# A third score bank, a deeper ring of weight loads, and work issued in another order, in a hybrid attention block

## Chip, cores and metric

One core of one Trainium2 chip runs the whole kernel. The metric is device time in microseconds (us), the median over runs. TensorE is the matrix engine, VectorE, ScalarE and GpSimd (POOL in the profile) work on tiles, SyncE (SP) issues most transfers.

## What is computed

```python
# D_MODEL 1024, SEQ 1024 + 16 meta tokens = L 1040, 8 heads of 64, float32
h    = rmsnorm(concat(meta, x), norm_g)
proj = h @ w_in      # u_pool, z_pool (512 each), q, k, v, z_attn (512 each), f_logit (8), g_pool, g_attn (1024 each)
y_pool = causal_multiscale_pool(u_pool, pool_w, pool_scale) * silu(z_pool)   # windows 2, 4, 8, 16
log_f  = log_sigmoid(f_logit + b_forget)
# logit[t, s] = q_t.k_s / 8 + sum of log_f over s < j <= t, causal, softmax over s
y_attn = forgetting_attention(q, k, v, log_f) * silu(z_attn)
merged = sigmoid(g_pool) * (y_pool @ w_up_pool) + sigmoid(g_attn) * (y_attn @ w_up_attn)
out = rmsnorm(x + merged @ w_out, final_norm_g)          # meta positions dropped
```

## The kernel before

Every float32 product is made of three: operands are split into a high and a low part (`hh`/`hl` for the activations, `whi`/`wlo` or `gw` for weights), and high x high, high x low and low x high are added up in one PSUM bank. A weight is loaded into a raw tile by SyncE's queue, copied to its high part by ScalarE (L157, L973) and subtracted to its low part by GpSimd or VectorE (L159, L978, L975).

**Attention stage.** There are 16 units: 4 pairs of heads (p), 2 heads of a pair (e), 2 halves of the queries. A unit of the first half has 5 blocks of 128 keys, one of the second half 9. `Unit.qk(b)` makes a score block: two products into a bank `ps` (L691, L692), VectorE adds bias and mask where the causal edge cuts the block (L698), ScalarE adds the bias elsewhere (L700), and VectorE keeps a running maximum (L705). `maxes` turns the maximum round (L710 to L723). `Unit.soft(b)` subtracts it (L732), exponentiates (L733), splits the result into `ph` and `pl` (L736, L737) and, two blocks later, `av` multiplies with V (L753). The score blocks of unit i + 1 are merged with the softmax blocks of unit i, so a phase holds either 5 softmax and 9 score blocks or 9 and 5.

Between these steps TensorE is given projections from a list, the fill (class `Fill`, `F.pull(ns)`): must-do ones (q, k and v of the next pair, `f_q`, `f_k`, `f_v`, `v_blocks`, with a `gate` that names the first unit in which they may start, and `apart`, which lets one go only behind a free one) and free ones (`f_u`, `f_raw`, results to DRAM through `st`, L343 and L353). `merged` pulls, after every step, `PACE * dve - pe` ns of fill, where the steps' `dve` is the planner's cost formula. A fill product is 24 matmuls into one bank of the pool `pj` (L171; V's transposes, L301, take a bank too); it is emptied by ScalarE and VectorE (L258/L262 for q, L281/L285 for k, L290 for v, L310/L311 for V's blocks). TensorE's order is the order of the program; the other engines' queues are ordered by a scheduler ahead of time, and each engine works through its queue in order. PSUM has 8 banks: `pj` 3, `psT` 2, `psS` 2 (scores), `psO` 1.

While attention runs, SyncE and GpSimd also add weight blocks in DRAM (`SUMS`, `put`, `add`) for the next stage. Behind unit 13 the first weights of that stage are loaded (`g_raw0`, L590), behind unit 14 they are split (L830, L833).

**Seven-product stage.** z_attn, z_pool and 512 columns of g_attn are projected by a two-by-two block scheme that takes seven block products (n = 0 to 6) of sums of blocks in place of eight; each has six column tiles i of 128, so there are 42 products in the list `order` (L1016). In the loop over `order`, step x splits the weights of product x + 4 (`split_next`, `w_split`), issues product x + 2 (`g_prod`), runs `before`, empties product x - 1 (`evict`: copies L1021, additions L1027, GpSimd additions L137, silus L1024), and runs what the table `extra` lists for it: sums of the softmax denominators (`acc_sum`, L934, L935, loads L929), `sums_in`, `sums_out`, steps of the pooling sums (`pool_chain`, L905), loads of attention results (`attn_in`) and of their reciprocals (`rc_in`, L883), `attn_norm` (L886), `h_split`, `pool_split` (L919, L920). In this loop all engines keep the order of the program. A raw weight tile holds two products' columns (`pair_in`, L961); two are in flight, and the next is loaded when both halves of one are split. The last four products alternate with `pool_mm`, the pooling mixer's product, whose banks come from the pool `p8`. The up projections (L171 again) and the output product (L1317) follow.

Of the kernel before, what the change touches and what calls it, by code (L numbers as in the profile page):

```python
# [8 lines left out]
F32 = mybir.dt.float32  # L9
# [13 lines left out]
KB = 128  # L23
# [8 lines left out]
HALVES = ((0, 512), (512, 1024))  # L32
PJ, PT = 3, 2
PACE = 1.0
LATENCY = 1800.0
# [20 lines left out]
def tile_hybrid_block(ctx, tc, x, meta, norm_g, w_in, b_forget, pool_w, pool_scale,  # L56
# [109 lines left out]
    def g_mm3(ps, terms):  # L166
# [3 lines left out]
        for i, (a, b) in enumerate(seq):  # L170
            nc.tensor.matmul(ps, a, b, start=(i == 0), stop=(i == len(seq) - 1))  # L171
            yield mm_ns(n)

    def g_proj(w, t0, t1):
        wh, wl = w
        ps = pj.tile([128, 512], F32, name="pj")[:, :t1 - t0]
        yield from g_mm3(ps, [(wh[:, k, :], wl[:, k, :], hh[k][:, t0:t1], hl[k][:, t0:t1]) for k in range(KO)])
        return ps
# [117 lines left out]
    def v_blocks(p, *parts):  # L296
        pt = pj.tile([128, 4, 2, 64], F32, name="pj")
        n = 0
        for b0, b1 in parts:
            for b in range(b0, b1):  # L300
                nc.tensor.transpose(pt[:, n], VT[p][:, KS[b]:KS[b] + KB], ident)  # L301
                n += 1
                yield 109.0
        for e in range(2):
            n = 0
            for b0, b1 in parts:
                pv = pt[:, n:n + b1 - b0]
                n += b1 - b0
                vh = V[p, e][:, b0:b1, e, :]
                nc.scalar.activation(vh, pv[:, :, e, :], AF.Copy)  # L310
                nc.vector.tensor_tensor(V[p, e][:, b0:b1, 1 - e, :], pv[:, :, e, :], r32(vh), op=ALU.subtract)  # L311
# [156 lines left out]
    for n, (kind, t0, t1) in enumerate(todo):  # L468
# [187 lines left out]
    class Unit:  # L656
# [9 lines left out]
        def a_steps(self):  # L666
            for b in range(self.nb):
                w = 512 - self.c0[b]
                yield w, 1.05 * w + 165 + 300 * (b * KB + KB > self.t0), 2 * mm_ns(w), (lambda b=b: self.qk(b))

        def c_steps(self):
            for b in range(self.nb):
                w = 512 - self.c0[b]
                yield w, 2.6 * w + 376, 2 * mm_ns(w), (lambda b=b: self.soft(b))

        def qk(self, b):
            p, e, q0, t0, kb, c0 = self.p, self.e, self.q0, self.t0, self.kb[b], self.c0[b]
# [12 lines left out]
            k0 = KS[b]  # L690
            nc.tensor.matmul(ps[:kb, c0:], ka[:, k0:k0 + kb], qa[:, q0 + c0:q0 + 512], start=True, stop=False)  # L691
            nc.tensor.matmul(ps[:kb, c0:], ka[:, k0:k0 + kb], ql[:, q0 + c0:q0 + 512], start=False, stop=True)  # L692
            nb_ = negc[:kb, b, h:h + 1]
            f0 = max(d1, c0)
            if d1 > c0:
                j = t0 + c0 - b * KB
                mk = tail if own_keys else mask[:, j:j + d1 - c0]
                nc.vector.scalar_tensor_tensor(s[:kb, c0:d1], ps[:kb, c0:d1], nb_, mk, op0=ALU.add, op1=ALU.add)  # L698
            if f0 < 512:
                nc.scalar.activation(s[:kb, f0:], ps[:kb, f0:], AF.Identity, bias=nb_)  # L700
# [107 lines left out]
    for i, u in enumerate(units):  # L808
# [40 lines left out]
    def bank():  # L849
        cnt[0] += 1  # L850
        return (pj if cnt[0] % 2 else p8).tile([128, 512], F32, name="pj")

    cnt = [0]
# [104 lines left out]

    def pair_in(n, q):
        raw_w[n, q] = wp.tile([128, 4, 256], F32, name="graw", tag="raw")  # L960
        nc.sync.dma_start(raw_w[n, q], rows_of(gsrc(n, q)))  # L961

# [35 lines left out]

    ga_ = [pool.tile([128, 512], F32, name=n) for pool, n in ((pj, "pj"), (pj, "pj"), (pj, "pj"), (psT, "pt"))]
    gb_ = [pool.tile([128, 512], F32, name=n) for pool, n in ((p8, "pj"), (p8, "pj"), (p8, "pj"), (psT, "pt"))]  # L1000
# [27 lines left out]

    later = []

# [10 lines left out]
    def evict(e):  # L1041
        n, i = e
        ps = onto[e]
        if i < 4:
# [53 lines left out]
    pair_in(*pairs.pop(0))  # L1098
    h_in(2)
# [6 lines left out]
    def split_next(e):  # L1106
        w_split(e)
        q = e[0], "aabbgg"[e[1]]
        halves[q] = halves.get(q, 0) + 1
        if halves[q] == 2 and pairs:  # L1110
            pair_in(*pairs.pop(0))

# [7 lines left out]
    def pad_hq():  # L1120
        hq.tile([128, SEQ], F32, name="wpad", tag="w")
        hq.tile([128, SEQ], F32, name="pad", bufs=1)

    def steps_of(g):
        return lambda: next(g, None)
# [6 lines left out]
    extra = {  # L1132
        (0, 0): [lambda: acc_sum(0), lambda: u_in(1)],
        (0, 1): [lambda: acc_sum(1), lambda: h_in(3)],
        (0, 2): [lambda: acc_sum(2), lambda: u_in(0)],
        (0, 3): [lambda: acc_sum(3)],
        (0, 5): [lambda: acc_sum(4)],
        (1, 1): [lambda: acc_sum(5), lambda: attn_in(0)],
        (1, 4): [lambda: acc_sum(6), lambda: attn_in(1)],
        (1, 5): [lambda: acc_sum(7), sums_in],  # L1140
        (2, 0): [lambda: h_split(3), lambda: h_in(5), lambda: attn_in(2)],
        (2, 1): [steps_of(c2_), lambda: attn_in(3)],
        (2, 2): [steps_of(c2_), sums_out],
        (2, 3): [steps_of(c2_)],
        (2, 4): [steps_of(c2_)],
        (2, 5): [steps_of(c1_), lambda: rc_in(0), lambda: rc_in(1)],
        (3, 0): [steps_of(c1_)],
        (3, 1): [lambda: h_split(4), lambda: h_in(6)],
        (3, 2): [steps_of(c1_), steps_of(c0_)],
        (3, 3): [steps_of(c0_), lambda: pool_split(3)],  # L1150
        (3, 4): [lambda: attn_norm(0)],
        (3, 5): [lambda: pool_split(2)],
        (4, 1): [lambda: h_split(5)],
        (4, 3): [lambda: pool_split(1)],
        (4, 4): [lambda: rc_in(2)],
        (5, 3): [lambda: h_split(6), lambda: attn_norm(1), lambda: rc_in(3)],
        (5, 2): [lambda: attn_norm(2)],
        (5, 1): [lambda: attn_norm(3), lambda: silu(za[0][:, T0_], za[0][:, T0_])],
        (5, 0): [lambda: pool_split(0), lambda: silu(za[1][:, T0_], za[1][:, T0_])],
        (5, 4): [lambda: silu(za[2][:, T0_], za[2][:, T0_]), lambda: silu(za[3][:, T0_], za[3][:, T0_])],  # L1160
    }
# [3 lines left out]
    for x, e in enumerate(order[:38]):  # L1165
# [7 lines left out]
        for f in before.get(e, ()):  # L1173
            f()
        if x:
            evict(order[x - 1])
# [39 lines left out]

    ws, rows_ = {}, {}
    ws[0, 0] = up_weights(0, 0)
    for n, i in enumerate((3, 2, 1, 0)):
# [88 lines left out]
    bk = [pool.tile([128, 512], F32, name=n) for pool, n in  # L1308
          ((pj, "pj"), (pj, "pj"), (pj, "pj"), (psT, "pt"), (p8, "pj"), (p8, "pj"), (p8, "pj"), (psT, "pt"))]
    ba, bb_ = bk[:4], bk[4:]  # L1310
# [126 lines left out]
```

## Time and profile before

| | us |
|---|---|
| median of 3 runs | 755.03 (754.86 to 755.35) |
| the profiled execution | 757.81 |
| its span, first to last instruction | 756.1 |
| TensorE busy | 720.1 |
| VectorE, ScalarE, GpSimd busy | 522.1, 425.5, 328.5 |
| attention stage, first to last score product | 82.9 to 414.3 |
| seven-product stage, first to last product | 446.3 to 585.6 |
| output product | 672.7 to 749.1 |

The first part of the profile's page gives the busy time of each engine; the list of waits names, for an engine's idle time, the instruction that ended it. A line of a timeline has start, length, engine, line, operation, output<-inputs and count, and in brackets the idle time ahead of it and what ended that. PE is TensorE, DVE VectorE, ACT ScalarE, SPq SyncE's queue.

### The profile page before, as it was taken

The page shows a single profiled execution, that of the slowest core. Times are in us where ns is not written, and L with a number is a line of the kernel's source. Part 1 is how long each engine was busy: PE and PEld are TensorE (multiplying, and loading weights), DVE is VectorE, ACT ScalarE, POOL GpSimd, SP SyncE. Part 2 cuts the span into 40 slices and gives each one's busy share as a digit, 9 for nine tenths or more (in the row PEclk, how much of TensorE's full clock was granted, in tenths as well). Part 3 has the DMA queues.
Part 4 walks back from the last instruction along what each step waited for, and adds up shares of the span by engine and source line. Part 5 has one row for each costly group of instructions (what it writes and reads, how often), then busy time and mean ns, then how long its engine had stood idle before and what let it go on. Part 6 is the DMA issues. An engine that isn't in the chain of part 4 may idle for free. (4 is left out here: it accounts for less than half of the span.)

```text
span 756.1 us, 10866 instructions
## 1 busy us (share of the span) xinstructions
PE 720.1 (95%) x3613; PEld 613.7 (81%) x3613; DVE 522.1 (69%) x917; ACT 425.5 (56%) x944; POOL 328.5 (43%) x417
## 2 busy tenths in 40 slices
PE   9999999999999999899996999999859999999996
PEld 6997989998979879797885888877737888888885
DVE  5643667786886868877773967767466744787775
ACT  7653576676866768676664634335343623526355
POOL 5422238485474845475464743335516001005243
PEclk9999999999999999999998999999988999999999
DMA  9211226958959597767787869685333656672006
GB/s 305 50 29 29 56 77 211 276 177 206 312 133 290 141 256 196 182 168 206 173 223 206 203 216 340 214 263 172 98 98 125 237 190 229 216 278 91 0 1 222
DMA packets 97226, 134.08 MB, mean 177 GB/s; under 512 B 11569, under 2 KB 62769, under 8 KB 94914
## 3 DMA queue, kind: packets, MB, share of 16 engines
q1 hardware_dynamic: 93360, 112.42, 46.6%
q0 software_dynamic: 2512, 18.35, 12.9%
q10 hardware_dynamic: 1298, 2.63, 0.9%
q8 instruction: 28, 0.46, 0.2%
q14 instruction: 28, 0.23, 0.1%
HBM read 103.29 MB, written 62.59 MB: 219 GB/s over the span
## 5 line engine op out<-in xcount | busy, mean ns | idle before, releaser
L171 PE MATMUL pj<-hh,whi 128*128 128x512 f32 (+3 forms) x576 | 130.1, 353 | 0.2 <-DVE V L311 0.2
L171 PE MATMUL pj<-hh,wlo 128*128 128x512 f32 (+3 forms) x576 | 129.6, 348 | 0.1
L171 PE MATMUL pj<-hl,whi 128*128 128x512 f32 (+3 forms) x576 | 128.6, 346 | 0.0
L171 PEld LDWEIGHTS pj<-hh,whi 128*128 128x128 f32 x576 | 98.3, 192 | 10.8 <-PE pj L301 0.4
L171 PEld LDWEIGHTS pj<-hh,wlo 128*128 128x128 f32 x576 | 96.3, 189 | 9.3 <-POOL wlo L435 0.3
L159 POOL TENSOR_TENSOR wlo<-raw,whi 128x256 fp32r<-128x256 f32 x100 | 75.5, 794 | 64.9 <-ACT whi L157 25.4
L171 PEld LDWEIGHTS pj<-hl,whi 128*128 128x128 f32 x576 | 96.0, 188 | 8.8
L737 DVE TENSOR_TENSOR pl<-S,ph 128x512 fp32r<-128x512 f32 (+4 forms) x112 | 87.0, 792 | 11.2 <-ACT ph L736 10.5
L745 POOL TENSOR_TENSOR acc<-acc,S 128x272 f32<-128x272 f32 (+4 forms) x80 | 77.5, 969 | 15.9 <-ACT S L733 11.1
L978 POOL TENSOR_TENSOR gw<-graw,gw 128x256 fp32r<-128x256 f32 x52 | 46.1, 910 | 70.9 <-ACT gw L973 56.9
L1016 PE MATMUL pj<-gh,gw 128*128 128x512 f32 x276 | 66.8, 397 | 5.0 <-ACT gw L973 2.4
L705 DVE TENSOR_TENSOR pt<-pt,S 128x400 f32<-128x400 f32 (+2 forms) x96 | 46.8, 487 | 33.8 <-ACT S L700 31.3
L700 ACT ACTIVATE S<-ps,negc 128x400 f32<-128x400 f32 (+2 forms) x96 | 48.7, 515 | 33.2 <-DVE S L698 31.5
L1016 PEld LDWEIGHTS pj<-gh,gw 128*128 128x128 f32 x276 | 51.5, 188 | 19.0 <-ACT gw L973 3.7
L736 ACT ACTIVATE ph<-S 128x512 fp32r<-128x512 f32 (+4 forms) x112 | 52.4, 480 | 8.8 <-PE po L753 7.7
L733 ACT ACTIVATE S<-S 128x512 f32<-128x512 f32 (+4 forms) x112 | 50.1, 478 | 10.6 <-DVE S L732 10.5
L691 PE MATMUL ps<-qa,ka 128*128 128x512 f32 (+4 forms) x112 | 37.9, 338 | 14.3 <-ACT S L700 14.1
L732 DVE TENSOR_TENSOR S<-S,pt 128x512 f32<-128x512 f32 (+4 forms) x112 | 50.5, 498 | 0.6
L973 ACT ACTIVATE gw<-graw 128x512 fp32r<-128x512 f32 x38 | 23.3, 624 | 39.7 <-DMA graw<-gs 19.0
L1211 DVE TENSOR_TENSOR rl<-pj,rl 128x512 f32<-128x512 f32 x32 | 21.9, 689 | 26.7 <-PE pj L171 26.0
L691 PEld LDWEIGHTS ps<-qa,ka 128*128 128x128 f32 x112 | 21.4, 191 | 21.2 <-ACT S L700 18.9
L692 PE MATMUL ps<-ql,ka 128*128 128x512 f32 (+4 forms) x112 | 38.1, 340 | 0.0
(239 smaller groups left out, 1396.0 us busy)
## 6 DMA issues: line engine op xcount, KB each, us to landing
raw<-in_w_in_dram SPq DMA_DIRECT2D x27, 512.0 KB, 4.5
gs<-gs POOLq DMA_DIRECT2D x4, 1536.0 KB, 11.4
graw<-gs SPq DMA_DIRECT2D x12, 512.0 KB, 4.0
gs<-in_w_in_dram SPq DMA_DIRECT2D x5, 1024.0 KB, 9.9
td<-in_w_out_dram SPq DMA_DIRECT2D x5, 1024.0 KB, 12.9
graw<-in_w_in_dram SPq DMA_DIRECT2D x9, 512.0 KB, 6.3
xt<-in_x_dram SPq DMA_DIRECT2D x8, 512.0 KB, 7.2
accd<-acc SPq DMA_DIRECT2D x16, 256.0 KB, 3.4
```

What stands on the lines that cost most here:

```text
L159: ins = nc.gpsimd.tensor_tensor(lo[:, k:k + 2], raw[:, k:k + 2], r32(hi[:, k:k + 2]), op=ALU.subtract)
L171: nc.tensor.matmul(ps, a, b, start=(i == 0), stop=(i == len(seq) - 1))
L691: nc.tensor.matmul(ps[:kb, c0:], ka[:, k0:k0 + kb], qa[:, q0 + c0:q0 + 512], start=True, stop=False)
L700: nc.scalar.activation(s[:kb, f0:], ps[:kb, f0:], AF.Identity, bias=nb_)
L705: nc.vector.tensor_tensor(m[:kb, c0:], m[:kb, c0:], s[:kb, c0:], op=ALU.max)
L732: nc.vector.tensor_tensor(s[:kb, c0:], s[:kb, c0:], self.pm[:kb, c0:], op=ALU.subtract)
L733: exps.append(nc.scalar.activation(s[:kb, c0:], s[:kb, c0:], AF.Exp))
L736: nc.scalar.activation(ph[:kb, c0:], s[:kb, c0:], AF.Copy)
L737: dves.append(nc.vector.tensor_tensor(pl[:kb, c0:], s[:kb, c0:], r32(ph[:kb, c0:]), op=ALU.subtract))
L745: accs.append(nc.gpsimd.tensor_tensor(acc[:kb, c0:], acc[:kb, c0:], s[:kb, c0:], op=ALU.add))
L978: nc.gpsimd.tensor_tensor(op[:, 1, k:k + 2], raw[:, k:k + 2], r32(op[:, 0, k:k + 2]), op=ALU.subtract)
L1016: nc.tensor.matmul(ps, stat(n, i, p, k), op_h[n][q][k // 2][:, k % 2], start=fresh and m == 0, stop=m == 11, skip_group_check=True)
```

## The change

Banks: `pj` has 2 banks, a new pool `pk` has 1. Every third score block takes `pk`, two of three `psS`. Before the attention stage the fill takes `pk` at every third product; in it (`spare[0] = False`), the fill has the 2 banks of `pj`. The pools of the later stages take `pk` where they took the third bank of `pj`.

Attention: ScalarE's part of a score block is issued ahead of VectorE's masked part. `PACE` and the planner's formulas have other constants. `f_k` is `apart`. `g_raw0` is loaded behind unit 12.

Seven-product stage: weight loads are issued whenever a raw tile is free (`pairs_in`); from step (2, 0) on there are two more raw tiles, in the space of the `hq` pool. The silus of `zp` are issued some steps later (`defer`; `run_due(x)` stands in step x between `before` and `evict`). The denominators' sums, the steps of the pooling sums, `attn_in`, `rc_in`, `attn_norm` and the silus of `za` stand at other steps.

```diff
-PJ, PT = 3, 2
-PACE = 1.0
+PJ, PT = 2, 2
+PACE = 1.05
...
+    pk = ctx.enter_context(tc.tile_pool(name="pk", bufs=1, space=PS))
...
+    turn, spare = [0], [True]
+    def third(pool, name):
+        turn[0] += 1
+        if turn[0] % 3 == 0:
+            return pk.tile([128, 512], F32, name="pj")
+        return pool.tile([128, 512], F32, name=name)
+    def fill_bank():
+        return third(pj, "pj") if spare[0] else pj.tile([128, 512], F32, name="pj")
...
+    spare[0] = False
...
-                yield w, 1.05 * w + 165 + 300 * (b * KB + KB > self.t0), 2 * mm_ns(w), (lambda b=b: self.qk(b))
+                yield w, 0.8 * w + 110 + 250 * (b * KB + KB > self.t0), 2 * mm_ns(w), (lambda b=b: self.qk(b))
...
-                yield w, 2.6 * w + 376, 2 * mm_ns(w), (lambda b=b: self.soft(b))
+                yield w, 2.8 * w + 390, 2 * mm_ns(w), (lambda b=b: self.soft(b))
...
-            ps = psS.tile([128, 512], F32, name="ps")
+            ps = third(psS, "ps")
...
+            if f0 < 512:
+                nc.scalar.activation(s[:kb, f0:], ps[:kb, f0:], AF.Identity, bias=nb_)
             if d1 > c0:
                 ...
                 nc.vector.scalar_tensor_tensor(s[:kb, c0:d1], ps[:kb, c0:d1], nb_, mk, op0=ALU.add, op1=ALU.add)
-            if f0 < 512:
-                nc.scalar.activation(s[:kb, f0:], ps[:kb, f0:], AF.Identity, bias=nb_)
...
-            F.add(f"k{p}", f_k(p))
+            F.add(f"k{p}", f_k(p), apart=True)
...
-        if i == 13:
+        if i == 12:
             g_raw0 = [...]
...
-    def pair_in(n, q):
-        raw_w[n, q] = wp.tile([128, 4, 256], F32, name="graw", tag="raw")
-        nc.sync.dma_start(raw_w[n, q], rows_of(gsrc(n, q)))
+    room, homes = ["raw", "raw"], {}
+    def pairs_in():
+        while pairs and room:
+            e = pairs.pop(0)
+            homes[e] = tag = room.pop(0)
+            raw_w[e] = (wp if tag == "raw" else hq).tile([128, 4, 256], F32, name="graw", tag=tag)
+            nc.sync.dma_start(raw_w[e], rows_of(gsrc(*e)))
...
+    def defer(k, f):
+        due.append((clock[0] + k, f))
+    def run_due(x):
+        clock[0] = x
+        for d in [d for d in due if d[0] <= x]:
+            due.remove(d)
+            d[1]()
...
-                silu(zp[i][:, T0_], zp[i][:, T0_], -1.0)
+                defer(3, lambda: silu(zp[i][:, T0_], zp[i][:, T0_], -1.0))
...
-                silu(zp[i][:, T1_], zp[i][:, T1_], -1.0)
+                defer(1, lambda: silu(zp[i][:, T1_], zp[i][:, T1_], -1.0))
...
-        if halves[q] == 2 and pairs:
-            pair_in(*pairs.pop(0))
+        if halves[q] == 2:
+            room.append(homes[q])
+            pairs_in()
...
+    def more_room():
+        room.extend(("w", "w"))
+        pairs_in()
```

The table `extra`, step by step (c2, c1, c0 are steps of the pooling sums, one each):

| what | before | after |
|---|---|---|
| acc_sum 0 to 4 | (0,0) (0,1) (0,2) (0,3) (0,5) | (0,1) (0,2) (0,3) (0,4) (0,5) |
| acc_sum 5, 6, 7 | (1,1) (1,4) (1,5) | (1,4) (1,5) (2,0) |
| sums_in, sums_out | (1,5), (2,2) | (2,0), (2,4) |
| more_room | none | (2,0) |
| c2 | (2,1) (2,2) (2,3) (2,4) | (0,0) (0,1) (2,1) (2,2) |
| c1 | (2,5) (3,0) (3,2) | (2,2) (2,3) (2,4) |
| c0 | (3,2) (3,3) | (3,0) (3,2) |
| attn_in 0 to 3 | (1,1) (1,4) (2,0) (2,1) | (1,1) (1,5) (2,1) (2,4) |
| rc_in 2, 3 | (4,4) (5,3) | (4,2) (4,4) |
| attn_norm 1 | (5,3) | (4,0) |
| silu of za 0, 1, 2, 3 | (5,1) (5,0) (5,4) (5,4) | (5,0) (5,4) (5,4) (6,4) |

More of the change, by code (lines that the diff above doesn't have):

```diff
@@ L296, in v_blocks @@
     def v_blocks(p, *parts):
-        pt = pj.tile([128, 4, 2, 64], F32, name="pj")
+        pt = fill_bank().rearrange("p (n e d) -> p n e d", e=2, d=64)
         n = 0
@@ L850, in bank @@
         cnt[0] += 1
-        return (pj if cnt[0] % 2 else p8).tile([128, 512], F32, name="pj")
+        return ((pj, p8, pj, p8, pk, p8)[cnt[0] % 6]).tile([128, 512], F32, name="pj")
     cnt = [0]
@@ L997, in stat @@
         return op_w[n, i][:, p, k]
-    ga_ = [pool.tile([128, 512], F32, name=n) for pool, n in ((pj, "pj"), (pj, "pj"), (pj, "pj"), (psT, "pt"))]
+    ga_ = [pool.tile([128, 512], F32, name=n) for pool, n in ((pj, "pj"), (pj, "pj"), (pk, "pj"), (psT, "pt"))]
     gb_ = [pool.tile([128, 512], F32, name=n) for pool, n in ((p8, "pj"), (p8, "pj"), (p8, "pj"), (psT, "pt"))]
@@ L1027, in plus_ @@
         return nc.vector.tensor_tensor(dst, ps, dst if a is None else a, op=ALU.add)
-    later = []
+    later, due, clock = [], [], [0]
+    def defer(k, f):
[5 more added lines that the diff above has]
+            d[1]()
     def g_store(j, half, src):
@@ L1142, in tile_hybrid_block @@
[L1142 to L1147, printed above, removed]
+        (0, 0): [steps_of(c2_), lambda: u_in(1)],
+        (0, 1): [steps_of(c2_), lambda: acc_sum(0), lambda: h_in(3)],
+        (0, 2): [lambda: acc_sum(1), lambda: u_in(0)],
+        (0, 3): [lambda: acc_sum(2)],
+        (0, 4): [lambda: acc_sum(3)],
@@ new lines, in tile_hybrid_block @@
+        (0, 5): [lambda: acc_sum(4)],
+        (1, 1): [lambda: attn_in(0)],
+        (1, 4): [lambda: acc_sum(5)],
+        (1, 5): [lambda: acc_sum(6), lambda: attn_in(1)],
+        (2, 0): [more_room, lambda: acc_sum(7), lambda: h_split(3), lambda: h_in(5), sums_in],
+        (2, 1): [steps_of(c2_), lambda: attn_in(2)],
+        (2, 2): [steps_of(c2_), steps_of(c1_)],
+        (2, 3): [steps_of(c1_)],
+        (2, 4): [steps_of(c1_), sums_out, lambda: attn_in(3)],
+        (2, 5): [lambda: rc_in(0), lambda: rc_in(1)],
@@ L1156, in tile_hybrid_block @@
-        (5, 3): [lambda: h_split(6), lambda: attn_norm(1), lambda: rc_in(3)],
+        (4, 4): [lambda: rc_in(3)],
+        (5, 3): [lambda: h_split(6)],
         (5, 2): [lambda: attn_norm(2)],
-        (5, 1): [lambda: attn_norm(3), lambda: silu(za[0][:, T0_], za[0][:, T0_])],
-        (5, 0): [lambda: pool_split(0), lambda: silu(za[1][:, T0_], za[1][:, T0_])],
-        (5, 4): [lambda: silu(za[2][:, T0_], za[2][:, T0_]), lambda: silu(za[3][:, T0_], za[3][:, T0_])],
+        (5, 1): [lambda: attn_norm(3)],
```

28 lines of the change are left out of this document (13 added, 15 removed).

## The prediction

> **What bounds the kernel now.** I read the page first, then the list of who waited for whom on TensorE, then a table of windows round each long wait, then the timelines of the five engines there. The page says that TensorE is the bound.
>
> ```profile
> span 756.1 us, 10866 instructions
> ...
> PE 720.1 (95%) x3613; PEld 613.7 (81%) x3613; DVE 522.1 (69%) x917; ACT 425.5 (56%) x944; POOL 328.5 (43%) x417
> ```
>
> No edit takes a matmul away, so only TensorE's idle time and its slow time can be won: 36 us idle, some of it before the first and behind the last matmul. The waits of TensorE, in total us, times and longest, show where it lies.
>
> ```profile
> PE ps L691 <- ACT S L700: 14.1, 9, 6.5
> PE pj L171 <- DVE gx L1027: 7.2, 1, 7.2
> PE pj L1016 <- ACT gw L973: 2.4, 2, 1.5
> PE pj L1016 <- DVE gx L1027: 1.5, 1, 1.5
> ...
> PE pj L1016 <- DVE zp L1027: 1.2, 1, 1.2
> ...
> PE pj L171 <- DVE V L311: 0.2, 1, 0.2
> ```
>
> Three places: score products (L691) that wait for ScalarE to empty a score bank, 14.1 us; the seven-product stage (L1016), 5.1 us; and one wait of 7.2 us at its end, before the pooling product (L171, pool_mm). Each large wait is followed by a stretch at half clock (the column after POOL's is the granted clock).
>
> ```profile
> 227.80:231.00 3.20, 3.18 (x9) 2.80 (x10) 2.10 (x3) 2.82 (x5) 1.86 (x4) 0.50 1.08 214
> 404.40:408.50 4.10, 4.10 (x10) 3.23 (x11) 2.08 (x3) 3.17 (x5) 4.10 (x7) 0.50 0.24 74
> 566.30:572.30 6.00, 5.98 (x14) 4.65 (x15) 1.72 (x3) 0.63 (x1) 5.57 (x8) 0.50 0.27 87
> ```
>
> Work done at 0.50 loses half of its stretch: 1.6, 2.0 and 3.0 us. So waits and clock together hold 33.2 us: 14.1 + 3.6 in attention, 12.3 + 3.0 in and just behind the product stage, 0.2 in the fill.
>
> **The change, part by part.**
>
> *First weights of the product stage loaded after unit 12, not 13.* The longest score wait is not about score banks:
>
> ```profile
> 392.70 0.40 SPq L590 DMA_DIRECT2D graw<-in_w_in_dram  x1
> ...
> 402.71 1.06 ACT L830 ACTIVATE gw<-graw 128x1024 fp32r<-128x1024 f32 x1 [5.76 <-DMA graw<-in_w_in_dram]
> 404.40 0.79 PE L691 MATMUL ps<-qa,ka 128*128 128x512 f32 x1 [6.55 <-ACT S L700]
> ```
>
> ScalarE's queue holds the copy L830 ahead of score evictions; it stands 5.76 us for a load issued 10 us before, and TensorE then stands 6.55 us. One unit earlier is some 20 us (next fence: 20.4 and 22.2 us for two units), twice the load's 10 us. The two loads pass unit 13's stores on SyncE's queue, 0.40 us of issue each, with nothing urgent behind them. The tiles they take belonged to pair 2, which is over. Gain 6.55 + 2.0 = 8.6 us.
>
> *Third score bank.* psS keeps two banks and every third tile goes to the new pk. Of the 14.1 us, 7.6 us in eight waits remain as true bank waits; the largest of them lie in the phases that run a short unit's softmax (5 blocks) beside a long unit's scores (9).
>
> ```profile
> 225.06 0.67 ACT L700 ACTIVATE S<-ps,negc 128x512 f32<-128x512 f32 x1
> 227.09 0.67 ACT L700 ACTIVATE S<-ps,negc 128x512 f32<-128x512 f32 x1
> 225.78 0.50 PE L691 MATMUL ps<-qa,ka 128*128 128x512 f32 x1 [1.32 <-ACT S L700]
> 227.82 0.79 PE L691 MATMUL ps<-qa,ka 128*128 128x512 f32 x1 [1.06 <-ACT S L700]
> ...
> 218.05:238.46 20.41, 18.03 (x83) 15.47 (x83) 13.27 (x29) 12.76 (x32) 11.01 (x15) 0.92 0.98 260
> 238.46:260.61 22.15, 22.15 (x122) 19.56 (x121) 18.24 (x36) 16.06 (x43) 14.79 (x15) 1.00 0.60 153
> ```
>
> Score 3 starts as eviction 1 ends (225.73), score 4 as eviction 2 ends (227.76). With three banks score 3 goes at once (225.78 - 1.32 = 224.46), and score 4, due about 0.7 us behind it (three products; eight take 1.98 us in the row at 353.17 below), is held by eviction 1 until 225.73: near 0.6 us instead of 2.4 here, 0.4 more if the shorter fill between scores is counted. Scaled to 7.6 us I leave 2.2. Gain 5.4 us and the 1.6 us of clock that came with 2.4 us of waits: 7.0 us, between 0 (ScalarE stays late at every block) and 9.2.
>
> The Trainium skill (TensorE: Matmul & The Clock Gate, HAM oscillation — how this bites in real kernels) says that the clock falls when TensorE idles longer than about 3.4 us. The first clock row disagrees: waits of 1.32 and 1.06 us were enough. By the page that 1.6 us would not hang on these waits, the gain would be 5.4 us and the time 734.5; I follow the row.
>
> *ScalarE ahead of the mask.* Both engines read the same bank.
>
> ```profile
> L700 ACT ACTIVATE S<-ps,negc 128x400 f32<-128x400 f32 (+2 forms) x96 | 48.7, 515 | 33.2 <-DVE S L698 31.5
> ```
>
> ScalarE now waits 31.5 us for VectorE's mask. Afterwards the mask waits for ScalarE, but the maximum follows it on VectorE with no further change of engine. The bank comes free after the same two operations, so I book 0 directly; the cover is VectorE's idle time (13.27 of 20.41 us busy, 18.24 of 22.15). If that is gone, the mask's wait moves into VectorE's queue and delays `pl` and the AV products.
>
> *Fill keeps two banks instead of three.* This is the price. A fill product may now start only when the last but one is emptied. Pairs of rows of the timeline: a product's first matmuls, and the last step of the eviction that would hold them.
>
> ```profile
> 77.55 0.60 ACT L258 ACTIVATE qa<-pj 64x512 fp32r<-64x512 f32 x1 [0.76 <-DVE ql L262]
> 77.95 1.37 PE L171 MATMUL pj<-hh,whi 128*128 128x384 f32 x7
> ...
> 160.26 0.50 PE L171 MATMUL pj<-hh,whi 128*128 128x272 f32 x2
> 161.54 0.48 ACT L290 ACTIVATE vt<-pj 128x384 f32<-128x384 f32 x1
> ...
> 210.59 0.85 PE L171 MATMUL pj<-hh,whi 128*128 128x512 f32 x3
> 212.34 0.56 DVE L285 TENSOR_TENSOR ka<-pj,ka 64x384 fp32r<-64x384 f32 x1
> ...
> 241.91 1.26 PE L171 MATMUL pj<-hh,whi 128*128 128x272 f32 x8
> 241.97 0.49 ACT L290 ACTIVATE vt<-pj 128x384 f32<-128x384 f32 x1
> ...
> 353.17 1.98 PE L171 MATMUL pj<-hh,whi 128*128 128x512 f32 x8
> 353.48 0.58 ACT L343 ACTIVATE st<-pj 128x512 f32<-128x512 f32 x1
> ```
>
> Overlaps: 0.20, 1.76, 2.31, 0.55, 0.89 us. The first and last pair are the first and last of 16 such in the attention stage; they add to 16.5 us, nearly all behind K's third piece and round V's short transposes. That is the upper end. The lower end takes the least lag seen (241.91: 0.55) at the three V's and nothing else: 2.5 us with the shorter overlaps behind them. Fewer banks cannot gain. `apart` on K puts a free product between Q and K and removes two (3.1 us), leaving 13.4. The rest comes in clusters, where a first wait lets ScalarE catch up before the second, and ScalarE loses its mask waits: I take 7 us, a bit over half.
>
> *Pace.* Per head the plan's sums go from 3736 + 6547 (scores) and 5374 + 12203 (softmax) to 3019 + 5201 and 5999 + 13658 ns: 27,860 against 27,877. The fill lasts as long; 0.7 us of it per unit moves from short-softmax to long-softmax phases. Cost 0, covered by VectorE's idle time above.
>
> *Product stage.* In its third column of products one weight load was late and nothing recovered.
>
> ```profile
> 488.89 1.93 SPq L944 DMA_DIRECT2D fin<-sums  x4
> ...
> 492.71 0.43 SPq L961 DMA_DIRECT2D graw<-gs  x1
> 500.67 0.63 ACT L973 ACTIVATE gw<-graw 128x512 fp32r<-128x512 f32 x1 [11.43 <-DMA graw<-gs]
> ...
> 551.82 0.63 ACT L1024 ACTIVATE zp<-zp 128x512 f32<-128x512 f32 x1 [6.02 <-DVE zp L1027]
> 557.16 1.49 DVE L886 TENSOR_TENSOR y<-y,rc 128x1024 f32<-128x1024 f32 x1 [2.86 <-DMA rc<-recs]
> 566.32 0.79 PE L171 MATMUL pj<-plh,pwh 128*128 128x512 f32 x1 [7.21 <-DVE gx L1027]
> ...
>   POOL zp L137: 12.1, 4
>   DVE zp L1027: 11.5, 4
> ```
>
> The load at 492.71 stood behind the softmax sums on SyncE and behind a two-buffer ring; ScalarE idled 11.43 us for it. From (2,0) on, two more raw tiles let loads run four products further ahead; what waits behind sums_in then is not needed for 10 us or more. The silus held ScalarE 12.1 + 11.5 us (last two rows, ScalarE's idle time before L1024), with the next weight splits queued behind them; issued three products (zp's first half) or one (second half) later, they find their sums ready. rc_in(2) and rc_in(3) move two products ahead and attn_norm(1), which frees the tile that rc_in(3) takes, six; so the 2.86 us for rc go. One silu of za moves from (5,1) to (5,0), one to (6,4): the same 0.6 us each, later in ScalarE's queue. The sums go one to two products later and the pool chains earlier on VectorE, with no instruction added; POOL's queue keeps its order. The chain that kept VectorE from emptying gx's bank, and pool_mm from starting, is made of these waits. Of 12.3 + 3.0 us I leave 1.8: VectorE gets the last sums, h_split(3) and both pool chains within five products. Gain 13.5 us, between 5.1 (the waits named L1016 alone) and 15.3. The other banks (ga_, bk, bank) keep their number.
>
> **Sum.** The profiled execution took 757.81 us (span 756.1 and 1.7 round it): 757.8 - 8.6 - 7.0 + 7.0 - 13.5 = 735.7. The median of the three runs, 755.03, stands 2.8 us lower; so 732.9.
>
> **The rivals.**
>
> *Bank cycling in the fill.* The 16.5 us are paid in full and two clusters trip the clock as at 227.8 (1.6 us each): 732.9 + 9.5 + 3.2 = 745.6. For it: the evictions' order is fixed in advance; only 0.2 us of fill wait appeared with three banks. Against: `apart` and ScalarE's freed 31.5 us. The Trainium skill, same page (A second HAM failure mode: psum-queue depth-cycling), tells of a kernel whose short idles at each bank change kept tripping the clock; the first clock row agrees that short waits can.
>
> *The product stage keeps its wait.* VectorE falls behind at (2,0) to (2,4), the bank for (3,2) is late again (1.5) and half of 7.2 + 3.0 stays: 6.6 instead of 1.8, 737.7.
>
> *The swap only turns the wait round.* VectorE, standing for ScalarE, delays evictions as much as the bank saves: 9.2 instead of 2.2 remain, 739.9. The Trainium skill (PSUM — Partial Sum Buffer, PSUM bank collisions raise a hardware error) has two engines on one bank kept apart in time whichever comes first; the 31.5 us row agrees.
>
> *All of it works.* Fill 2.5, nothing left in scores or products: 732.9 - 4.5 - 2.2 - 1.8 = 724.4.
>
> *Slower.* The fill's bank waits must exceed 29 us, the 29.1 of gains; with every overlap doubled because ScalarE's new order puts evictions last, 33 us: 758.9. Nothing but the fixed order speaks for it.
>
> **How the numbers follow.** Forecast 0.45 (728 to 738), bank cycling 0.20, product stage 0.13, swap 0.08, all of it 0.11, slower 0.03. 722 to 748 reaches over all but the last and the tails. A measurement of this kernel tells 0.2% (1.5 us) from no change; nothing but a mix of all mishaps lands there: 0.02; faster 0.95.
>
> **What would show it.** Right: no L830 wait above 1 us; L691's waits under 3 us in total; L171 waiting 4 to 10 us for L290, L285, L310/L311 or L343; pool_mm starting with no 7 us wait and no 0.50 clock behind it; no ScalarE idle before L1024. Wrong: L171's waits above 12 us, a new long wait of ScalarE for a load, or L1016 still waiting for gx.

## The result and the profile after

The changed kernel takes 741.9 us (median; 741.8 to 742.77 in four runs) against 755.19 for the kernel before beside it: a ratio of 0.982 (95% interval 0.981 to 0.984), 13.3 us less. The profiled execution took 742.0 for a span of 740.3. The prediction said 732.9, in a range of 722 to 748: faster, as forecast, inside the range, and 9.0 us above the point. Most of those 9.0 us is one stall that no term of the sum stood for: 8.9 us by its own trace, 6.8 to 7.6 by a run without it (both below).

The page of the changed kernel, first the span and the busy time of the engines, shows that TensorE is still the bound and busier by two points. Its line numbers are higher than before: the score products are now L704 and L705, ScalarE's and VectorE's halves of the eviction L709 and L713, the fill products L172, the product stage L1034.

```profile
span 740.3 us, 10889 instructions
...
PE 714.7 (97%) x3613; PEld 612.2 (83%) x3613; DVE 521.7 (70%) x917; ACT 426.3 (58%) x944; POOL 336.2 (45%) x417
```

The list of TensorE's waits (total us, times, longest), which the prediction was made from, now reads:

```profile
PE ps L704 <- ACT S L709: 7.1, 2, 6.8
PE pj L172 <- ACT vt L302: 5.1, 4, 2.1
PE pj L172 <- ACT st L355: 1.8, 3, 0.8
...
PE po L766 <- DVE pl L750: 1.0, 1, 1.0
PE pj L172 <- ACT qa L270: 0.8, 1, 0.8
...
PE pj L313 <- DVE V L323: 0.3, 1, 0.3
...
PE pj L172 <- DVE ka L297: 0.2, 1, 0.2
```

Read it against the list of before. No row of L1034, gw, gx or zp is left, and none of pool_mm (L172 behind gx): 12.3 us of waits in the product stage are gone. Nine score waits (14.1 us) have become two, and one of these two is 6.8 us long: the score banks otherwise hold TensorE for 0.3 us. In their place the fill waits for its banks: 5.1 + 1.8 + 0.8 + 0.3 + 0.2 = 8.2 us. A table of windows shows the product stage of before and after, and the stretch round the one long wait (columns: length, then busy time of PE, PEld, DVE, ACT and POOL, then granted clock, DMA share, GB/s). The first row is of the kernel before, the others of the changed one.

```profile
486.00:580.00 94.00, 81.75 (x335) 64.17 (x334) 54.95 (x59) 39.83 (x63) 44.75 (x52) 0.95 0.50 143
```

```profile
138.24:142.37 4.13, 0.00 (x1) 0.00 (x0) 0.00 (x0) 0.08 (x1) 0.00 (x0) 1.00 0.89 290
142.37:149.19 6.82, 4.19 (x12) 3.99 (x13) 4.17 (x6) 6.82 (x16) 4.20 (x6) 0.50 0.87 288
...
486.00:580.00 94.00, 94.00 (x407) 76.39 (x406) 70.64 (x76) 51.95 (x78) 53.90 (x52) 1.00 0.69 207
```

In the changed kernel the stage's last product starts at 569.8, so the last 10 us of its row belong to what follows. Over the whole stretch TensorE now works through 94 us of 94, at full clock. At 138.24 every engine stands still while the DMA engines are 0.89 busy; then TensorE works 4.19 us at half clock, which loses 2.1. With the wait of 6.8 that makes 8.9 us. The timeline of the changed kernel says who started it (start, length, engine, line; idle time ahead and its end in brackets):

```profile
130.44 1.07 POOL L611 DMA_DIRECT2D hs<-hsl  x1
130.53 0.38 SPq L153 DMA_DIRECT2D raw<-in_w_in_dram  x1
131.00 1.02 SPq L367 DMA_DIRECT2D sp_u<-st  x2
...
142.29 0.40 ACT L365 ACTIVATE st<-pj 128x272 f32<-128x272 f32 x1 [8.00 <-DMA sp_u<-st]
145.00 0.80 PE L704 MATMUL ps<-qa,ka 128*128 128x512 f32 x1 [6.76 <-ACT S L709]
```

The tile `st` of the u fill has two buffers. ScalarE's copy of the third piece of a u row (L365) needs the first buffer back, whose store to `sp_u` was issued at 131.00 and landed only at 142. ScalarE's queue holds the steps of the softmax and the score evictions behind that copy. VectorE stands 8.49 us for ScalarE's `ph`, GpSimd 8.38 us for its exponentials, and TensorE for a score bank. The DMA view of these 1.3 us of issues (KB each, us to landing) and that of 135 to 139, by queue (packets, MB, share of the 16 engines), show why:

```profile
hs<-hsl POOLq DMA_DIRECT2D x1, 1024.0 KB, 11.6
raw<-in_w_in_dram SPq DMA_DIRECT2D x1, 512.0 KB, 4.2
sp_u<-st SPq DMA_DIRECT2D x2, 192.0 KB, 11.0
```

```profile
q0 software_dynamic: 85, 0.70, 92.9%
q1 hardware_dynamic: 87, 0.13, 10.8%
```

From 135 to 139 GpSimd's queue (q0) sends 85 packets of 8 KB each, the accumulating add of the h state (L611), and SyncE's queue (q1) sends 87 of 1.5 KB, the store: one for one. The add takes 92.9% of the engines' time and the store crawls at its pace. The Trainium skill (DMA: Bandwidth & Descriptors, Queues, rings and completion order) says that a DMA engine takes turns between the queues that have work, a packet at a time; the 85 against 87 agree with that. The 11.0 us fit it, as a small transfer with small packets then gets a small share.

The add did not act alone. Its first packet goes out only at about 133.6, 3.2 us after its issue, and until 133.5 SyncE's queue has sent 0.38 MB, less than the 512 KB load that was issued at 130.53 ahead of the store. So it seems that the store still stood behind that load when the add's packets began.

### The profile page after: what moved, and what is told of

Its sections match the earlier page's. It is cut to its first block, busy times and chain, and to the rows that moved or that the text cites. A ratio compares the mean times of both kernels' runs of the same rounds, so it can differ in the third digit from the quotient of the medians.

```text
span 740.3 us, 10889 instructions
## 1 busy us (share of the span) xinstructions
PE 714.7 (97%) x3613; PEld 612.2 (83%) x3613; DVE 521.7 (70%) x917; ACT 426.3 (58%) x944; POOL 336.2 (45%) x417
## 4 chain that ended last, share of the span: by engine, by line
PE 72%; ACT 9%; DVE 7%; DMA 2%; issue 2%; POOL 1%; POOLq 0%; SPq 0%; ACTq 0%; DVEq 0%
PE pj L172 38%; PE pj L1034 12%; PE pj L1354 8%; PE pt L1034 4%; PE po L766 4%; PE pt L1354 2%; ACT S L746 2%; DMA sp_u<-st 2%; ACT ph L749 1%; PE ps L705 1%; PE ps L704 1%; ACT S L709 1%; PE pj L529 1%; DVE pl L750 1%; DVE S L745 1%
## 5 line engine op out<-in xcount | busy, mean ns | idle before, releaser
L172 PE MATMUL pj<-hh,whi 128*128 128x512 f32 (+3 forms) x576 | 130.5, 354 | 7.9 <-ACT vt L302 5.1
L172 PE MATMUL pj<-hh,wlo 128*128 128x512 f32 (+3 forms) x576 | 129.1, 348 | 0.3 <-POOL wlo L447 0.3
L172 PE MATMUL pj<-hl,whi 128*128 128x512 f32 (+3 forms) x576 | 128.0, 346 | 0.0
L172 PEld LDWEIGHTS pj<-hh,whi 128*128 128x128 f32 x576 | 96.8, 191 | 20.7 <-ACT vt L302 6.3
L172 PEld LDWEIGHTS pj<-hh,wlo 128*128 128x128 f32 x576 | 97.1, 190 | 9.5 <-POOL wlo L447 0.5
L172 PEld LDWEIGHTS pj<-hl,whi 128*128 128x128 f32 x576 | 96.5, 188 | 9.2
L996 POOL TENSOR_TENSOR gw<-graw,gw 128x256 fp32r<-128x256 f32 x52 | 50.0, 984 | 47.6 <-ACT gw L991 45.2
L1034 PE MATMUL pj<-gh,gw 128*128 128x512 f32 x276 | 65.8, 395 | 0.0
L1034 PEld LDWEIGHTS pj<-gh,gw 128*128 128x128 f32 x276 | 52.0, 188 | 12.2
L709 ACT ACTIVATE S<-ps,negc 128x512 f32<-128x512 f32 (+4 forms) x63 | 31.8, 517 | 13.1 <-PE ps L705 12.6
L766 PE MATMUL po<-pl,V 128*128 128x512 f32 (+4 forms) x112 | 37.6, 335 | 1.0 <-DVE pl L750 1.0
L756 POOL TENSOR_TENSOR acc<-S 128x400 f32<-128x400 f32 (+1 forms) x16 | 20.9, 1306 | 37.9 <-ACT S L746 33.1
L1354 PE MATMUL pj<-opw 128*128 128x512 f32 (+1 forms) x168 | 36.2, 374 | 0.0
## 6 DMA issues: line engine op xcount, KB each, us to landing
gs<-gs POOLq DMA_DIRECT2D x4, 1536.0 KB, 13.5
td<-in_w_out_dram SPq DMA_DIRECT2D x5, 1024.0 KB, 12.7
```

The source lines that it names most:

```text
L766: nc.tensor.matmul(self.po[:, c0:], v, r[:kb, c0:], start=(b == 0 and i == 0), stop=(b == self.nb - 1 and i == 1))
L996: nc.gpsimd.tensor_tensor(op[:, 1, k:k + 2], raw[:, k:k + 2], r32(op[:, 0, k:k + 2]), op=ALU.subtract)
L1034: nc.tensor.matmul(ps, stat(n, i, p, k), op_h[n][q][k // 2][:, k % 2], start=fresh and m == 0, stop=m == 11, skip_group_check=True)
L1354: nc.tensor.matmul(ps, pick(A_, k, p)[:, i * 128:(i + 1) * 128], pick(B_, k, q)[:, c0:c1], start=start and n == 0, stop=n == 11, skip_grou ...
```

## The experiments

Each time is compared with the kernel before on the same chip: its median is 755.78 us beside the first four kernels below, 755.19 beside the next four, 755.79 beside the last four. Between these groups the ratios are to be compared.

**Moving the add.** The theory was that the add, put in flight 0.56 us ahead of the store, causes the stall.

```diff
-        1: [(add, HS["11"], HS["l11"]), (n21, 0), (put_g, GS[1], GB["11"])],
-        2: [(n21, 1), (put_g, GS[5], GB["12"])],
+        1: [(n21, 0), (put_g, GS[1], GB["11"])],
+        2: [(add, HS["11"], HS["l11"]), (n21, 1), (put_g, GS[5], GB["12"])],
```

> The changed kernel with one step moved: GpSimd's accumulating add of the h state (hs<-hsl) is issued in the fill of unit 2 instead of unit 1. Theory (the store of the second u piece landed 11 us after its issue because that add was put in flight ahead of it, and ScalarE's next copy stood 8.00 us for its landing): the store lands within about 3 us, the 6.76 us wait of TensorE near 138 us and the half clock behind it go, 742 - 9 = 733. Rival (the store is late because SyncE issues it late, behind the raw-weight load, and because of the three rearranging stores beside it): the wait of ScalarE stays at 5 us or more and the time at 740 to 742. If the add only makes the same trouble one unit later, the stall moves and the time stays near 742 too.

Measured: 735.13 us, ratio 0.972 (0.970 to 0.975) against 0.982: by this one move 6.8 us of the 9 come back by the medians, 7.6 by the ratios (1.0% of 755). ScalarE's wait and the landing of the stores issued in the same stretch:

```profile
135.57 0.40 ACT L365 ACTIVATE st<-pj 128x272 f32<-128x272 f32 x1 [2.15 <-DMA sp_u<-st]
```

```profile
sp_u<-st SPq DMA_DIRECT2D x2, 192.0 KB, 6.6
```

The wait of 8.00 is 2.15, TensorE's 6.76 is 0.90, and the clock stays full. The theory holds for most of it. The rival has a part: with no add in flight the store still needs 6.6 us, right behind a 512 KB load on SyncE (issued at 129.66, the store at 130.14) and with the next transfers of 256 to 1024 KB behind it. How much of the 6.6 belongs to each is not shown.

**The parts of the change, one at a time on the kernel before.** Loading the product stage's first weights after unit 12 (`if i == 12`):

> The kernel before with one edit: the first weights of the product stage are loaded after unit 12, not 13. Theory: the 5.76 us wait of ScalarE for graw and the 6.55 us wait of TensorE near 398 us go, with the half clock behind them: 755 - 8.6 = 746.5. Rival (the wait goes, but TensorE then stands for the next bank of the same unit, so that half comes back): 750 to 751.

Measured: 748.32, ratio 0.991 (0.988 to 0.994), 7.5 us less. The weight load's wait is gone, and of its 6.55 us on TensorE 0.6 return as other score waits (14.1 - 6.55 = 7.6 are now 8.2). The theory holds, a little short.

```profile
PE ps L691 <- ACT S L700: 8.2, 9, 1.6
```

The whole product-stage part (raw buffers, later silus, table of side steps):

> The kernel before with only the changes of the product stage (two more raw buffers from column 2 on, activations issued later, sums, softmax and pool steps at other products). Theory: all 12.3 us of waits and the 3.0 us of half clock in and just behind the stage go, as the trace of the changed kernel shows none: 755 - 15.3 = 740. By the prediction 13.5 go: 741.5. Rival (the waits went because the attention stage ended otherwise, so that engines came into the stage with another lead): under 10 us go, 745 or more.

Measured: 739.7, ratio 0.979 (0.977 to 0.982), 16.1 us less. No wait of L1021 (the product stage in this kernel) or pool_mm is left in the list; its first row is the untouched attention stage. So this part stands by itself: its gain comes although the attention stage keeps its waits.

```profile
PE ps L691 <- ACT S L700: 13.9, 9, 6.4
```

The banks alone (third score bank, two banks for the fill, none of the swap, the pace or `apart`):

> The kernel before with only the bank change: a third score bank, and two banks for the fill. Theory by the prediction's two terms: 7.0 us of gain at the scores, 7.0 of loss in the fill, 755 +/- 1.5. By the sizes in the trace of the changed kernel (0.35 us of score waits and 8.2 of fill waits left): 755 - 9 + 8 = 754. Rival (the bank alone does not help while ScalarE waits for the mask): score waits stay above 5 us beside the fill's 8, 760 or more. Rival (the fill's two banks cost less without the new order): under 750.

Measured: 756.41, ratio 1.001 (0.9998 to 1.003): no change. The list shows an exchange.

```profile
PE pj L172 <- ACT vt L302: 4.6, 4, 1.7
PE pj L704 <- ACT S L713: 4.5, 1, 4.5
PE pj L172 <- ACT qa L270: 2.9, 2, 2.2
...
PE pj L172 <- DVE ka L297: 2.0, 2, 1.6
PE pj L172 <- ACT st L355: 1.8, 3, 0.8
```

The one score wait left, 4.5 us, is the late weight load. All 7.6 us of true bank waits are gone without the swap, and 4.6 + 2.9 + 2.0 + 1.8 = 11.3 us of fill waits have come. If their gains add, the three parts give -7.5 - 16.1 + 0.6 = -23.0 us; the whole change gave -13.3. So the swap, the pace and `apart`, with what they did to the order, would cost 9.7 on top. The stall is 6.8 to 7.6 of that. As `apart` by itself saves 3.0 us (below), some 5 us remain that no single run accounts for. The gains of the first weights and of the banks overlap, as the late load holds TensorE for 4.5 us here and not 6.55; that is one part of it, and the new costs of the planner may be another (2.4 us, below).

**The swap.** On the changed kernel, VectorE's mask ahead of ScalarE again:

```diff
-            if f0 < 512:
-                nc.scalar.activation(s[:kb, f0:], ps[:kb, f0:], AF.Identity, bias=nb_)
             if d1 > c0:
                 ...
+            if f0 < 512:
+                nc.scalar.activation(s[:kb, f0:], ps[:kb, f0:], AF.Identity, bias=nb_)
```

> The changed kernel with VectorE's mask ahead of ScalarE's eviction again. TensorE's and SyncE's orders stay. The third-bank run left no wait of a score bank without the swap, but 11.3 us of fill waits. Theory (the swap brings nothing at the score banks and spares the fill some 3 us of its waits): score waits stay under 1 us, fill waits go from 8.2 to about 11, so 745 if the stall near 138 us stays and 736 if it goes. By the prediction (0 directly): 742, or 733 without the stall. Rival (the swap was needed for the third bank once the pace is the new one): score waits of 3 us or more come back.

Measured: 743.3, ratio 0.984 (0.981 to 0.987) against 0.982: not told apart from no effect. The stall stays (the first row below, 6.6 of it), fill waits are 6.7 + 1.7 + 0.5 = 8.9 instead of 8.2, not 11, and score waits other than the stall total 0.6. The prediction's 0 is nearest; the 3 us of the theory did not show.

```profile
PE ps L704 <- ACT S L713: 7.2, 3, 6.6
```

**The pace.** The changed kernel with `PACE = 1.0` and the two old formulas:

> The changed kernel with the planner's costs of before (PACE 1.0 and the two old formulas). The stall near 138 us hung on a lead of 0.6 us: the add was issued at 130.44 and the store behind it at 131.00, while before had the store at 129.55 and the add at 131.31. Theory (the new pace shifted the second unit's phase by that much): the stall goes and the time falls to 733 +/- 2, as the pace itself is worth 0. Rival (the swap or the bank count shifted it): the stall stays, 742. If the pace carried part of the score gain, score waits above 1 us come back with the old costs and eat part of the 9.

Measured: 735.29, but its four executions took 740.96, 737.3, 730.5 and 733.28; ratio 0.973 (0.967 to 0.980). The timeline of the profiled one, first GpSimd, then SyncE:

```profile
131.02 1.04 POOL L611 DMA_DIRECT2D hs<-hsl  x1
```

```profile
130.19 1.01 SPq L367 DMA_DIRECT2D sp_u<-st  x2
```

The store goes 0.83 us ahead of the add, and TensorE's wait there falls to 1.6. So the new costs (the pace and the two formulas, which were not tried apart) are what put the two in the wrong order. Two other traces agree: with the banks alone, under the old costs, the store goes at 128.66 and the add at 130.41, and with the swap undone, under the new costs, the store goes at 130.56 and the add at 129.99. But the profiled execution, the slowest of the four, has a stall of the same kind at 250, 8.0 us before a fill product: ScalarE stood for the landing of a store of y while another accumulating add from GpSimd, issued at 239.12, was in flight. The DMA view gives that add, the timeline ScalarE's wait:

```profile
hsX<-hs POOLq DMA_DIRECT2D x1, 1024.0 KB, 11.4
```

```profile
248.67 0.60 ACT L777 ACTIVATE t<-po 128x512 f32<-128x512 f32 x1 [7.82 <-DMA sp_y<-t]
```

That the runs differ by 10 us would fit such an order decided by fractions of a microsecond; only one of them has a trace.

**`apart`.** The kernel with the moved add (735.13), without the rule:

> The changed kernel with the add issued one unit later (735.1) and without the rule that keeps K's fill apart. By the prediction, the rule spares two clusters of overlap, 3.1 us: fill waits go from 7.9 to about 11 and the time to 738. Rival (its place in the order is as good): 735.

Measured: 738.15, ratio 0.977 (0.973 to 0.980), 3.0 us more. The list shows the waits that `apart` spares, for `qa` and `ka`:

```profile
PE pj L172 <- ACT qa L270: 3.1, 2, 2.5
PE pj L172 <- DVE ka L297: 1.9, 1, 1.9
```

The time meets the forecast to a tenth of a microsecond, but that is luck. The intervals reach 1.7 and 2.6 us to each side, and the cost is made up otherwise than forecast. In the profiled executions TensorE is idle for 21.1 us instead of 19.7, so that most of the new waits are offset elsewhere, while it is busy for 716.3 instead of 712.6 us. Three stretches at half clock, from 86.0, 164.6 and 208.9, behind fill waits of 1.88, 2.11 and 2.51 us, are where it is slower; the run with the rule has none of these three. So what `apart` spares is in good part clock, for which the prediction had no term here.

**V's transposes in a score bank**, again on the kernel with the moved add. Of the fill waits left there, 5.1 us are for `vt`, most directly behind V's transposes, which hold the fill's other bank; the score banks had slack.

```diff
-        pt = fill_bank().rearrange("p (n e d) -> p n e d", e=2, d=64)
+        pt = (fill_bank() if spare[0] else third(psS, "ps")).rearrange("p (n e d) -> p n e d", e=2, d=64)
```

> The changed kernel with the add issued one unit later (735.1), and V's transposes written into a score bank instead of a fill bank. Theory (four fill products wait for ScalarE's vt copy because the short transposes hold the other bank; 5.1 us, of them 3.8 directly behind transposes): these 3.8 us go and no score wait appears, 731. Rival (the score banks have no slack in those phases): as much comes back as waits of L704 for S, 735 or more.

Measured: 728.0, ratio 0.963 (0.961 to 0.966), 7.1 less than 735.13 where 4 were expected (5.5 between the two profiled executions). The waits for `vt` and for `st` are both out of the list: the 3.8 us of the theory and 3 us more. In return score waits grow from 1.3 to 4.4 us, 2.5 of them for the transposes' own bank:

```profile
PE pj L704 <- DVE V L323: 2.5, 2, 2.3
```

**The product stage in three.** On the kernel before, first the two more raw buffers alone:

> The kernel before with only the two more raw buffers of the product stage from (2,0) on (and the first two loads issued together). The whole product-stage change gave -16.1 us. Theory (the late load is the root: ScalarE's 11.43 us for graw<-gs starts the chain, and VectorE's lateness at gx follows from it): ScalarE's waits for raw weights fall from 31.5 us to under 15, the waits L1016 for gw and part of pool_mm's go, 755 - 9 = 746. Rival (the silus that ScalarE waits 23.6 us for are the root, and the load is early enough once they move): 752 or more.

Measured: 748.9, ratio 0.991 (0.989 to 0.993), 6.9 less, between theory and rival. ScalarE's waits for raw weights fall to 17.4 us, not under 15, and its 20.6 us before the silus stay. Then the later silus alone:

```diff
-                silu(zp[i][:, T0_], zp[i][:, T0_], -1.0)
+                defer(3, lambda: silu(zp[i][:, T0_], zp[i][:, T0_], -1.0))
```

> The kernel before with only the silus of zp issued three products and one product later. Theory (raw buffers are the root): ScalarE's 23.6 us before the silus go, but it then stands for raw weights instead, since the ring still holds two: 755 - 4 = 751. Rival (the silus are the root): 742 to 746.

Measured: 744.51, ratio 0.985 (0.983 to 0.987), 11.3 less. Then the table alone:

> The kernel before with only the table of side steps changed (sums one to two products later, pool chains earlier, rc loads and attn_norm moved). Theory: VectorE's queue is cleared earlier, so that gx's bank is emptied earlier and pool_mm's 7.2 us shrink to about 4, with nothing won at the weights: 755 - 4 = 751. Rival (the table only makes room for the other two edits): 754 to 756. If all three are each enough to break the chain, each of the three runs gives over 10.

Measured: 750.49, ratio 0.993 (0.991 to 0.995), 5.3 less. The time and pool_mm's wait (4.2) are as the theory had them, but the waits for gw fell too, from 2.4 to 0.8. The waits of TensorE in the stage tell how far each went; the three lists, in the same order:

```profile
PE pj L171 <- DVE gx L1032: 5.6, 1, 5.6
...
PE pj L171 <- DVE zp L863: 1.0, 1, 1.0
```

```profile
PE pj L171 <- DVE zp L863: 2.3, 1, 2.3
...
PE pj L1021 <- DVE gx L1032: 1.1, 1, 1.1
```

```profile
PE pj L171 <- DVE gx L1032: 4.2, 1, 4.2
...
PE pj L171 <- DVE zp L863: 1.1, 1, 1.1
PE pj L1021 <- ACT gw L978: 0.8, 2, 0.4
```

Of 12.3 us, 6.6, 3.4 and 6.1 are left. Moving the silus gives the largest single gain, more than the load: with them moved, ScalarE stands longer for raw weights than before (27.4 + 12.7 us in the next fence, 19.0 + 12.5 before), and TensorE hardly waits. The two groups are those of the second kernel, the copies of weights and the silus of zp (the last three figures name what ended the idle time).

```profile
L978 ACT ACTIVATE gw<-graw 128x512 fp32r<-128x512 f32 x38 | 23.5, 626 | 48.4 <-DMA graw<-gs 27.4 <-DMA graw<-in_w_in_dram 12.7 <-DMA sp_y<-t 4.5
L1029 ACT ACTIVATE zp<-zp 128x512 f32<-128x512 f32 x8 | 5.0, 626 | 2.9 <-DVE zp L1032 2.9
```

And the three do not add: 6.9 + 11.3 + 5.3 = 23.5 us, 16.1 together. Each cuts into the same waits.

**The best version.** Moved add, V's transposes in a score bank, and the planner's old costs:

> The changed kernel with the add issued one unit later, V's transposes in a score bank (728.0) and the planner's costs of before. The old costs with the changed kernel gave 730.5 in the run without the long stall, against 735.1 where only the add was moved: theory (the new costs are worth nothing or a loss, once the banks hold): 724 to 728. Rival (a store of y is again caught behind the accumulating DMA of GpSimd near 240 us, or the new costs earn their place): 730 or more, with runs several us apart.

Measured: 725.61 (724.74 to 725.97), ratio 0.960 (0.958 to 0.962): the fastest kernel here, 30.2 us below the one before, and within the 724 to 728 of the theory. With the new pace it was 0.963 (0.961 to 0.966); the intervals overlap a little, so that the old costs are 2.4 us better is likely and no more. No stall behind an add appears in TensorE's list:

```profile
PE ps L704 <- DVE V L323: 1.9, 2, 1.4
PE pn L427 <- DVE car L564: 1.3, 1, 1.3
PE pj L704 <- DVE V L323: 1.0, 1, 1.0
```

TensorE is busy for 710.8 of its 723.8 us, and no wait beside these exceeds 0.5 us.

## Why the prediction came out as it did, step by step

*First weights: -8.6 forecast, -7.5 measured.* The mechanism is as written: the wait is gone, and so is the half clock behind it. The interval of the ratio, 4.6 to 9.4 us, holds the forecast; 0.6 us of other score waits came back.

*Third bank -7.0, fill with two banks +7.0: 0 forecast, +0.6 measured alone.* The +7.0 was meant with `apart`, the run of the banks alone is without it. Each term was too small by one to two us, and that the two errors nearly cancel is luck. The score banks keep 0.3 us, not 2.2; the fill waits 11.3 us without `apart` and 8.2 with it, not 7. The overlap method (every fill product whose bank would still be full, from the timeline of before) gave an upper end of 16.5, and 13.4 with `apart`; 68% and 61% of that came. `apart` itself was forecast at 3.1 and measured at 3.0, with half clock as a large part of it.

*The 1.6 us of clock in the third bank's term* rested on one row. The run with the earlier weights has the same two waits, and its clock stays whole:

```profile
225.90 0.50 PE L691 MATMUL ps<-qa,ka 128*128 128x512 f32 x1 [1.29 <-ACT S L700]
227.94 0.50 PE L691 MATMUL ps<-qa,ka 128*128 128x512 f32 x1 [1.08 <-ACT S L700]
```

```profile
227.94:231.30 3.36, 3.36 (x17) 3.04 (x18) 2.42 (x4) 2.95 (x6) 2.89 (x5) 1.00 1.11 225
```

So those waits can trip the clock and need not; the term was worth 0 to 1.6.

*The swap: 0 forecast, nothing measurable.* ScalarE's 31.5 us for the mask became 21.7 us of VectorE's for ScalarE in the changed kernel (VectorE's list of waits), nearly all of it off TensorE's path. What may reach TensorE is the wait for `pl`, 1.0 us in the changed kernel and out of the list with the swap undone: the delay that the prediction named for the case that VectorE's idle time is gone.

```profile
DVE S L713 <- ACT S L709: 21.7, 28, 1.8
```

*Product stage: -13.5 forecast, -16.1 measured.* The waits and clock named (15.3 us) all went. The 1.8 us left for VectorE's extra work at (2,0) to (2,4) did not come. The story in that step was half right: "one weight load was late and nothing recovered". That nothing recovered weighed more, by the run with the silus alone.

*Pace: 0 forecast.* This is the step that failed. "The fill lasts as long" holds for the plan's sums, and the step counted engine time only. It did not ask what moves past what in the queues of transfers. The new costs moved a load and a store on SyncE behind an add on GpSimd, whose order had hung on 1.76 us before (store 129.55, add 131.31, by the timeline of before) and on 0.56 us after. That stall is 6.8 to 7.6 of the 9.0 us between the point and the result; what is left of it after the move, and the gains that do not add, are the rest. Of the signs of a wrong prediction, "a new long wait of ScalarE for a load" came true with a store in the load's place. Of the signs of a right one, the score waits under 3 us did not come (7.1, of them 6.8 the stall), and ScalarE still idles 3.6 us before the silus; the others came. With the add moved, the kernel takes 735.1 against 732.9. That this is so close is partly luck, as the product stage gave 2.6 us more than its term and the parts together less than their sum.

*The rivals.* The swap's (739.9) was nearest in time and wrong in kind: 7.1 us of score waits remain where it had 9.2, but 6.8 of them are the stall, which stays with the swap undone. Bank cycling (745.6) is wrong for the changed kernel, with 8.2 us of fill waits and no half clock behind any of them; without `apart` its half clock does come. The product stage kept no wait.

What stays open: the some 5 us by which the parts give less together than one by one, beyond the stall. And the changed kernel's four executions agree within 1 us, and the one with the old pace spreads over 10; why that order is so much less steady was not tried.

## What to carry to other kernels

When an edit shifts a schedule, list the transfers it moves past each other, with their margins, above all small stores that free a double buffer and large accumulating adds on another queue: a margin of a microsecond is not one. A wait on a chain has several causes that each carry part of it; price such edits together and test them singly, as their gains do not add. And when one pool of banks is made smaller, ask which of its short users can go to the pool that has become slack; here that was worth more than the exchange itself.

## What the runs showed of the hardware

A store of 192 KB took 11.0 us beside a 1 MB accumulating add from GpSimd and 6.6 with no such add in flight, both right behind a 512 KB load. In the kernel before, a store issued at 131.28, 0.03 us ahead of the add, took 3.6: until 133.2 only SyncE's queue sent packets there, as the second fence shows.

```profile
sp_u<-st SPq DMA_DIRECT2D x1, 192.0 KB, 3.6
```

```profile
q1 hardware_dynamic: 971, 0.64, 107.6%
```

So some 2 us passed between the issue of that add and its first packet; it was 1.6 us in the run with the moved add and 3.2 in the changed kernel. Once the add's packets flow, in the changed kernel from 135 to 139, the two queues alternate by packet, 85 against 87, so the queue with 1.5 KB packets got 0.13 MB while the one with 8 KB packets got 0.70.

The same wait can trip the clock or not. The 2.1 us wait behind V's transposes did so in the run without `apart` (first row) and did not in the one with the moved add (second row, from the end of that wait):

```profile
164.60:168.00 3.40, 3.40 (x15) 3.20 (x14) 1.84 (x6) 1.30 (x3) 3.16 (x6) 0.50 0.85 231
```

```profile
162.45:166.00 3.55, 3.55 (x25) 3.46 (x26) 2.75 (x6) 1.77 (x5) 3.24 (x6) 1.00 1.00 291
```

The stretches at half clock came in sizes of 3.4 us (before, 227.6 to 231.0), 6.8 (the changed kernel, 142.4 to 149.2) and 10.2 (before, 562.1 to 572.3). The Trainium skill (TensorE: Matmul & The Clock Gate, What's actually happening) has the clock decided over free-running windows of 3413 ns; the sizes agree, and where a wait falls in such a window would explain why equal waits differ. No run here set that position, so this is not shown.
